# A changed opening: norms from token-major rows, modulation weights through GpSimd's queue, chains kept together, memory ahead of the context

## The chip, the core and the metric

The kernel runs on one core of a Trainium2 chip. A core has five engines that each work through their own list of instructions in order: TensorE (PE, matrix products), VectorE (DVE), ScalarE (ACT), GpSimd (POOL) and SyncE (SP, which here only issues DMAs). They wait for one another by semaphores. The metric is the device time of one execution in microseconds; lower is better. TensorE's clock as granted stands in the profile as a share of its full 2.4 GHz.

## The reference, cut to what matters

Two transformer-like blocks follow each other on 512 latent tokens of 1024 features, with 256 context tokens and 256 memory tokens:

```python
def first_block(x, c, ctx, c_ctx, ...):
    m_l = split(silu(c) @ ada_w + ada_b, 9)        # modulation of the latents
    m_c = split(silu(c_ctx) @ ada_w + ada_b, 9)    # modulation of the context
    x   = x   + 0.5 * m_l[2] * swiglu(modulate(rms_norm(x, norm1_w), m_l[0], m_l[1]), ffn1...)
    ctx = ctx + 0.5 * m_c[2] * swiglu(modulate(rms_norm(ctx, norm1_w), m_c[0], m_c[1]), ffn1...)
    y_l, y_c = token_mixing(...)                   # retention and gated linear attention
    x = x + m_l[5] * y_l
    x = x + 0.5 * m_l[8] * swiglu(modulate(rms_norm(x, norm3_w), m_l[6], m_l[7]), ffn2...)
    return rms_norm(x, final_norm_w)

def second_block(x, mem, ...):
    # dilated attention and a gated recurrence, then attention over the memory, then an MLP
    ... memory_cross_attention(rmsnorm(h, g), rmsnorm(mem, norm_mem_g), w_cq, w_ck, w_cv, w_co) ...

rms_norm(x, w) = x * rsqrt(mean(x * x over the features) + 1e-6) * w
```

The change concerns how the first block begins: the root-mean-square factors of x, ctx and mem, the modulation vectors (columns of `ada_w` times the activated condition), and the projections of the memory onto `w_ck` and `w_cv`, which the second block needs much later but which are made in the opening.

## The kernel before

All activations lie feature-major: eight tiles of 128 features by 512 (or 256) tokens. Every matrix product runs in three passes with operands split into a high and a low half (`wh`, `wl` of a weight; `hh`, `hl` of the latents, `h2` of the context and memory): high x high, high x low, low x high. ScalarE makes the high half by a copy, VectorE the low half by a subtraction (`split`, L446). A weight tile of 128x1024 is loaded by `wraw` (L434) on SyncE's queue into one of six places named `wr`, which all weights share; the modulation weights `ada_w` go there too.

The modulation: each 128 values of a modulation vector are one VectorE instruction (`tensor_tensor_reduce`, in the profile the custom instruction that writes `junk` and `mod`) over a 128x1024 tile of `ada_w` and the condition, which is replicated over partitions. `ada_first` (L655) does it for the first two vectors (shift and scale), 128 features at a time, and `ada` (L645) for the others.

The opening (L736 to L764) runs as follows. The condition, x and the memory are loaded. `rstd` (L526) finds the factors of a norm from the feature-major tiles: ScalarE squares them, VectorE adds the squares (`ss`), TensorE sums over the partitions by products with ones (`colsum`, into `st`), and VectorE computes the inverse root (`mean_eps` L516 and `rsqrt` L505: twelve small instructions one behind the other, `rsm`, `rsy`, `rst`). `spread` (L521) replicates the factors over partitions by TensorE (`rb`), and ScalarE copies them (`rbs`). `first_norm` (L708) takes eight steps, one per 128 features: two modulation products, the gain, `xn` = x times factor, the modulated halves `hh` and `hl`. After each step the up weights of FFN1 that have been loaded take the new features: seven units are begun in this loop (FIRST, L38). Two steps of the memory (`memory`, L679: four units of `w_ck`, two of `w_cv`) stand ahead of the loop and the rest behind it. Then FFN1 (`swiglu`, L810) goes on: for each up unit the latents' product, and from the seventh (ALONE, L37) also the context's; `ffn1_side` (L868) puts steps of other work beside each unit: `first_norm` of the context first, then the remaining modulation.

The order on each engine is not the order of the code. A planner (`Plan`, L143) records every operation with a cost and its dependences, and `issue` (L232) lists them: it takes the operation that can start first by its cost model, older ones first among equals, and keeps track of the places of each tile (`allowed`, L266; `pick`, L283). Every operation is put out by one line, so that nearly all of the profile's rows name L363.

Of the kernel before, what the change touches and what calls it, by code (L numbers as in the profile page):

```python
# [11 lines left out]
F32 = mybir.dt.float32  # L12
F32R = mybir.dt.float32r
I32 = mybir.dt.int32
# [4 lines left out]
P = 128  # L19
# [13 lines left out]
WBUFS = 5  # L33
TAIL = 3
# [108 lines left out]
class Plan:  # L143
# [9 lines left out]
    YIELD = 0.3  # L153

    def __init__(self, tc):
        self.tc, self.ops, self.caps, self.warm = tc, [], {}, False
# [13 lines left out]
    def add(self, name, engine, method, args, kwargs):  # L170
# [29 lines left out]
        self.ops.append((name, engine, method, args, kwargs, deps, tiles, cost, func))  # L200

    def cost(self, name, method, args, kwargs, outs, ins):
# [13 lines left out]
        if name == "SP":  # L216
            x = outs[0] if outs else ins[0]
            return int(np.prod(x.shape)) * 4 / 360.0 + 50
# [13 lines left out]
    def issue(self):  # L232
# [50 lines left out]
        def pick(e):  # L283
# [26 lines left out]
        while oldest < n:  # L310
# [5 lines left out]
            name, engine, method, args, kwargs, deps, tiles, cost, func = ops[i]  # L316
# [5 lines left out]
            landed = end + (2000 if e == "SP" else 0)  # L322
# [53 lines left out]
def tile_two_blocks(ctx: ExitStack, tc: tile.TileContext, a: dict, out: bass.AP, dbg=None):  # L376
# [128 lines left out]
    def rsqrt(m, cols):  # L505
        y = plan.tile(tp, [P, 32], F32, "rs_y", fresh("rsy"), 2)[:, :cols]
        t = plan.tile(tp, [P, 32], F32, "rs_t", fresh("rst"), 2)[:, :cols]
        V.tensor_scalar(y.bitcast(I32), m.bitcast(I32), 1, None, op0=ALU.logical_shift_right)
        V.tensor_scalar(y.bitcast(I32), y.bitcast(I32), -1, 0x5F3759DF, op0=ALU.mult, op1=ALU.add)
        for _ in range(3):  # L510
            V.tensor_mul(t, y, y)
            V.scalar_tensor_tensor(t, t, -0.5, m, op0=ALU.mult, op1=ALU.mult)
            V.scalar_tensor_tensor(y, t, 1.5, y, op0=ALU.add, op1=ALU.mult)
        return y

    def mean_eps(src, cols, scale):  # L516
        m = plan.tile(tp, [P, 32], F32, "rs_m", fresh("rsm"), 2)[:, :cols]
        V.tensor_scalar(m, src, scale, EPS, op0=ALU.mult, op1=ALU.add)
        return m
# [135 lines left out]
    def ada_first(c, s, k, junk):  # L655

        w = wraw(a["ada_w"][c, k], 1024)
# [21 lines left out]
    def memory():  # L679
# [81 lines left out]
    for _ in early:  # L761
        pass
    ctx_ = load(NC, "ctx", a["ctxT"])
    cond[1] = conditions(1)  # L764
# [901 lines left out]
def _arrange(inputs):  # L1666
# [3 lines left out]
    r["xT"], r["ctxT"], r["memT"] = _fm(g["x"][0]), _fm(g["ctx"][0]), _fm(g["mem_2"][0])  # L1670
# [81 lines left out]
```

## Time and profile before

| | |
|---|---|
| median of 3 runs | 2075.18 us (2071.36 to 2081.82) |
| the profiled execution | 2077.35 us |
| its span | 2075.5 us |
| TensorE busy | 2009.8 us, 97% |
| VectorE busy | 1190.4 us, 57% |
| ScalarE busy | 794.5 us, 38% |
| mean granted clock of TensorE | 0.981 |

The times are device times of whole executions; the profile is one more execution, and the span is the part of it between the first and last instruction. A row of the timeline gives the start, the length, the engine, the line, the operation, the tile written and the tiles read, and in brackets how long the engine had been idle ahead of it and what ended that.

### The profile page before, as it was taken

What the parts mean: (1) busy time and instruction counts of PE and PEld (TensorE: products, weight loads), DVE (VectorE), ACT (ScalarE), POOL (GpSimd) and SP (SyncE); (2) the same over time, 40 slices, a digit from 0 to 9 for tenths busy, and PEclk for the clock granted to TensorE, in tenths of its full rate; (3) what the DMA queues carried; (4) which work ended last, traced back from release to release, by engine and by line L of the source; (5) the groups of instructions that cost most, each with busy time, mean ns of one, the idle gap of its engine ahead of it and who ended that gap; (6) DMA issues with size and microseconds to landing.
All of it is one profiled execution on the core that took longest, in us unless ns stands there. A gap on an engine that the chain in (4) does not pass through costs nothing.

```text
span 2075.5 us, 27876 instructions
## 1 busy us (share of the span) xinstructions
PE 2009.8 (97%) x11033; PEld 1688.6 (81%) x11033; DVE 1190.4 (57%) x2157; ACT 794.5 (38%) x1238; POOL 121.1 (6%) x126
## 2 busy tenths in 40 slices
PE   5889999999999998999999999999998999999998
PEld 4779888888888876978988888888765888888887
DVE  7887844426247788589633333374866655343344
ACT  5452121221225654374432222343676363233231
POOL 0000000000000023110000000001243010000000
PEclk9989999999999999999999999999997999999999
DMA  8866624417132112232233323234321214333321
GB/s 312 270 236 199 196 77 140 145 60 224 51 107 94 45 52 72 67 91 83 71 117 101 97 92 104 86 94 124 85 74 27 64 59 132 101 92 102 93 70 41
DMA packets 73538, 225.57 MB, mean 109 GB/s; under 512 B 9360, under 2 KB 12096, under 8 KB 73408
## 3 DMA queue, kind: packets, MB, share of 16 engines
q1 hardware_dynamic: 73408, 223.80, 34.7%
q8 instruction: 86, 1.41, 0.3%
q14 instruction: 44, 0.36, 0.1%
HBM read 210.00 MB, written 5.24 MB: 104 GB/s over the span
## 4 chain that ended last, share of the span: by engine, by line
PE 87%; issue 5%; DVE 3%; DMA 2%; ACT 2%; POOL 1%; SPq 0%; DVEq 0%; ACTq 0%; POOLq 0%
PE p L363 77%; PE as L363 1%; PE gs L363 1%; PE ro L363 1%; PE rs L363 1%; PE at L363 1%; PE ao L363 1%; PE st L363 1%; PE go L363 1%; DVE junk L363 1%; DMA wr<-in_ffn_up_dram 1%; PE gl L363 1%; DVE rg_r L363 0%; PE rb L363 0%; POOL pg L363 0%
## 5 line engine op out<-in xcount | busy, mean ns | idle before, releaser
L363 ACT ACTIVATE wh<-wr 128x1024 fp32r<-128x1024 f32 (+4 forms) x295 | 298.2, 1012 | 751.1 <-PE p L363 566.1
L363 PE MATMUL p<-hh,wh 128*128 128x512 f32 (+1 forms) x1320 | 505.2, 389 | 13.2 <-ACT hh L363 7.9
L363 PE MATMUL p<-hl,wh 128*128 128x512 f32 (+1 forms) x1320 | 507.2, 388 | 0.0
L363 DVE TENSOR_TENSOR wl<-wr,wh 128x1024 fp32r<-128x1024 f32 (+4 forms) x295 | 345.9, 1177 | 170.7 <-ACT wh L363 77.6
L363 PE MATMUL p<-hh,wl 128*128 128x512 f32 (+1 forms) x1320 | 363.4, 387 | 4.3 <-DVE wl L363 4.3
L363 PE MATMUL p<-lo,wh 128*128 128x512 f32 (+1 forms) x831 | 310.0, 381 | 2.5 <-DVE lo L363 2.5
L363 PE MATMUL p<-hi,wh 128*128 128x512 f32 (+1 forms) x831 | 308.7, 380 | 2.0 <-ACT hi L363 2.0
L363 PEld LDWEIGHTS p<-hh,wh 128*128 128x128 f32 x1320 | 248.9, 190 | 57.6 <-ACT hh L363 10.4
L363 PEld LDWEIGHTS p<-hh,wl 128*128 128x128 f32 x1320 | 243.9, 190 | 54.5 <-DVE wl L363 4.7
L363 PEld LDWEIGHTS p<-hl,wh 128*128 128x128 f32 x1320 | 250.9, 191 | 37.5 <-issue 1.3
L363 PE MATMUL p<-hi,wl 128*128 128x512 f32 (+1 forms) x831 | 211.6, 375 | 0.0
L363 PEld LDWEIGHTS p<-lo,wh 128*128 128x128 f32 x831 | 158.6, 191 | 27.4 <-DVE lo L363 3.2
L363 PEld LDWEIGHTS p<-hi,wh 128*128 128x128 f32 x831 | 158.3, 191 | 24.4 <-ACT hi L363 2.2
L363 PEld LDWEIGHTS p<-hi,wl 128*128 128x128 f32 x831 | 148.8, 188 | 27.2
L363 PEld LDWEIGHTS p<-h,wh 128*128 128x128 f32 x816 | 138.8, 189 | 26.1
L363 DVE CUSTOM_DVE_ANT_0 junk<-wr,cond,vec 128x1024 f32<-128x1024 f32 x112 | 143.3, 1281 | 21.0 <-DMA wr<-in_ada_w_dram 20.1
L363 PE MATMUL p<-h,wh 128*128 128x256 f32 x816 | 145.5, 280 | 0.0
L363 DVE TENSOR_TENSOR act<-act,p 128x512 f32<-128x512 f32 (+1 forms) x68 | 38.3, 583 | 176.9 <-PE p L363 175.5
L363 DVE SCALAR_TENSOR_TENSOR x<-p,gate,x 128x512 f32<-128x512 f32 (+1 forms) x59 | 42.6, 723 | 106.0 <-PE p L363 106.0
L363 DVE TENSOR_TENSOR x<-p,x 128x512 f32<-128x512 f32 (+1 forms) x51 | 33.6, 658 | 112.9 <-PE p L363 112.7
L363 PE MATMUL p<-h,wl 128*128 128x256 f32 x408 | 97.3, 279 | 0.0
L363 PEld LDWEIGHTS p<-hid,wh 128*128 128x128 f32 x352 | 64.3, 188 | 14.3
(344 smaller groups left out, 2434.6 us busy)
## 6 DMA issues: line engine op xcount, KB each, us to landing
wr<-in_ffn_up_dram SPq DMA_DIRECT2D x100, 512.0 KB, 3.7
wr<-in_ada_w_dram SPq DMA_DIRECT2D x88, 512.0 KB, 4.4
wr<-in_mlp_up_dram SPq DMA_DIRECT2D x32, 512.0 KB, 3.6
wr<-in_mlp_dn_dram SPq DMA_DIRECT2D x32, 512.0 KB, 3.6
wr<-in_w_out_dram SPq DMA_DIRECT2D x16, 512.0 KB, 4.2
wr<-in_ffn_dn_dram SPq DMA_DIRECT2D x16, 448.0 KB, 3.2
wr<-in_ffn_dn_dram SPq DMA_DIRECT2D x16, 384.0 KB, 3.2
wr<-in_ffn_dn_dram SPq DMA_DIRECT2D x16, 320.0 KB, 2.8
```

Of the source, the lines that this page charges most:

```text
L363: ins = getattr(engine, method)(*args, **kwargs).ins
```

## The change

Token-major copies of x, ctx and mem are passed in beside the feature-major ones. `rstd_rows` loads 128 tokens at a time, and one ScalarE instruction squares a row and sums it (`accum_out`); VectorE's adds and TensorE's sums over ones are no longer needed for these three norms. The factor of x is computed first of all. `ada_w` tiles go through GpSimd's DMA queue into two places of their own (`wa`), and the weights keep four places `wr`. The chains of `rsqrt` and `mean_eps` are marked urgent for the planner. The memory's work moves from around the latents' loop to the sides of the first two FFN1 units, the context's loads and norm to the sides of the next three, and the remaining modulation behind them.

```diff
+RAWS = 4
+ARAWS = 2
...
+    RUSH = 200
+    LANDING = 2000
...
-        if name == "SP":
+        if method == "dma_start":
             x = outs[0] if outs else ins[0]
             return int(np.prod(x.shape)) * 4 / 360.0 + 50
...
+                rush = [c for c in cand if ops[c[1]][9] and c[0] - first <= self.RUSH]
+                if rush:
+                    return min(rush)
...
-    def wraw(ap, cols):
-        raw = plan.tile(wp, [P, 1024], F32, "wr", fresh("wr"), 6)
-        sync.dma_start(raw[:, :cols], ap)
+    def wraw(ap, cols, queue=sync, tag="wr", n=RAWS):
+        raw = plan.tile(wp, [P, 1024], F32, tag, fresh(tag), n)
+        queue.dma_start(raw[:, :cols], ap)
         return raw
+
+    def araw(c, j):
+
+        return wraw(a["ada_w"][c, j], 1024, G, "wa", ARAWS)
...
     def rsqrt(m, cols):
...
+        with plan.hurry():
+            V.tensor_scalar(y.bitcast(I32), m.bitcast(I32), 1, None, op0=ALU.logical_shift_right)
...
+    def rstd_rows(ap, n):
+
+        ss, junk = small(n // P, "ss"), wide4("junk")
+        for t in range(n // P):
+            S_.activation(junk, wraw(ap[t], 1024), AF.Square, accum_out=ss[:, t : t + 1])
+        return rsqrt(mean_eps(ss, n // P, 1.0 / D), n // P)
...
-            w = wraw(a["ada_w"][c, j], 1024)
+            w = araw(c, j)
...
-                y = rstd(mem.x)
+                y = rstd_rows(a["mem"], NC)
...
-    def first_norm(st):
-
-        rb = slot("rbs")[:, : st.n]
-        S_.activation(rb, rms_rstd(st.x), AF.Copy)
+    def first_factor(n, rows):
+        rb, made = bank("rb"), slot("rbs")[:, :n]
+        spread(rstd_rows(rows, n), n // P, rb)
+        S_.activation(made, rb[:, :n], AF.Copy)
+        return made
...
-    cond = [conditions(0), None]
+    latf = first_factor(NL, a["x"])
     lat = load(NL, "x", a["xT"])
     xt = lat.x
-    mem = load(NC, "mem", a["memT"])
-    early = memory()
-    for _ in range(2):
-        next(early)
-    normal = first_norm(lat)
+    cond = [conditions(0), None]
+    normal = first_norm(lat, latf)
...
-    for _ in early:
-        pass
-    ctx_ = load(NC, "ctx", a["ctxT"])
-    cond[1] = conditions(1)
+    mem = load(NC, "mem", a["memT"])
+    early = memory()
+    ctx_ = Stream(NC, None)
...
-    normal = first_norm(ctx_)
+    def second_norm():
+        ctx_.x = load(NC, "ctx", a["ctxT"]).x
+        factor = first_factor(NC, a["ctx"])
+        cond[1] = conditions(1)
+        yield from first_norm(ctx_, factor)
+
+    normal = second_norm()
...
-        if f < 4:
-            for _ in range(2):
+        if f < 2:
+            for _ in range(3 + f):
+                next(early, None)
+        elif f < ALONE - 1:
+            for _ in range(3):
                 next(normal, None)
-        else:
-            for _ in range(4 if f < 6 else 3):
+        if f >= ALONE - 2:
+            for _ in range(4):
                 next(rest, None)
```

How the instructions stand after it, in three places. First SyncE's queue behind the loads of x, before (`in_ada_w` are the modulation weights, `in_w_ck` the memory's weights, `in_ffn_up` those of FFN1):

```order
L363 DMA wr_132<-in_w_ck_dram 128x1024
L363 DMA wr_150<-in_w_ck_dram 128x1024
L363 DMA wr_168<-in_ada_w_dram 128x1024
L363 DMA wr_188<-in_ada_w_dram 128x1024
L363 DMA wr_219<-in_ffn_up_dram 128x1024
L363 DMA wr_245<-in_ffn_up_dram 128x1024
L363 DMA wr_263<-in_ada_w_dram 128x1024
L363 DMA wr_296<-in_ada_w_dram 128x1024
L363 DMA ctx_316<-in_ctxT_dram 128x512
```

The same queue behind the loads of x, now:

```order
L384 DMA cond_132<-in_cond_dram 128x1024
L384 DMA wr_137<-in_ffn_up_dram 128x1024
L384 DMA wr_145<-in_ffn_up_dram 128x1024
L384 DMA wr_152<-in_ffn_up_dram 128x1024
L384 DMA wr_162<-in_ffn_up_dram 128x1024
L384 DMA mem_169<-in_memT_dram 128x512
L384 DMA mem_179<-in_memT_dram 128x512
L384 DMA mem_181<-in_memT_dram 128x512
L384 DMA mem_189<-in_memT_dram 128x512
```

The modulation weights have left SyncE's queue, and the memory stands behind the first up weights. They are on GpSimd's queue now, from its start (MEMSET, ISA and AFFINE_SELECT make the identity matrix):

```order
masks.py:197 MEMSET ident_70 128x128
L384 DMA wa_81<-in_ada_w_dram 128x1024
masks.py:199 ISA
masks.py:199 AFFINE_SELECT ident_70<-ident_70 128x128
L384 DMA wa_85<-in_ada_w_dram 128x1024
L384 DMA wa_173<-in_ada_w_dram 128x1024
L384 DMA wa_187<-in_ada_w_dram 128x1024
```

Each load from the third on follows the instruction that has read the tile two before it. On VectorE, the first modulation products before (ISA rows that write `junk` are the products; `rst`, `rsy` end an inverse root, `ck` is the memory's projection):

```order
L363 TENSOR_TENSOR rst_280<-rsy_270 128x2
L363 SCALAR_TENSOR_TENSOR rst_280<-rst_280,rsm_265 128x2
L363 SCALAR_TENSOR_TENSOR rsy_270<-rst_280,rsy_270 128x2
L363 ISA junk_309,mod_310<-wr_168,cond_81,vec_79 128x1024
L363 ISA mod_310 128x1
L363 TENSOR_TENSOR ck_323<-p_185,fac_319 128x256
L363 TENSOR_TENSOR ck_323<-p_240,fac_319 128x256
L363 SCALAR_TENSOR_TENSOR gain_328<-mod_310,vec_79 128x1
L363 ISA junk_309,mod_332<-wr_188,cond_81,vec_79 128x1024
L363 ISA mod_332 128x1
L363 TENSOR_TENSOR xn_336<-x_83,rbs_321 128x512
L363 TENSOR_TENSOR wl_342<-wr_219,wh_278 128x1024
```

The same place on VectorE now:

```order
L384 TENSOR_TENSOR xn_154<-x_107,rbs_139 128x512
L384 TENSOR_TENSOR xn_156<-x_114,rbs_139 128x512
L384 TENSOR_TENSOR xn_158<-x_121,rbs_139 128x512
L384 ISA junk_164,mod_165<-wa_81,cond_132,vec_79 128x1024
L384 ISA mod_165 128x1
L384 SCALAR_TENSOR_TENSOR gain_171<-mod_165,vec_79 128x1
L384 ISA junk_164,mod_175<-wa_85,cond_132,vec_79 128x1024
L384 ISA mod_175 128x1
L384 TENSOR_TENSOR wl_183<-wr_137,wh_160 128x1024
L384 TENSOR_TENSOR wl_194<-wr_145,wh_167 128x1024
L384 TENSOR_TENSOR hl_206<-xn_141,hh_185 128x512
L384 ISA junk_164,mod_210<-wa_173,cond_132,vec_79 128x1024
```

The products of x and its factor (`xn`) stand ahead of the first modulation product, no other chain stands there, and a step holds two products that read the two places `wa`, then two low halves of weights and one of the latents (`hl`). Last, VectorE ahead of the context's units, before (`cond_81` and `cond_484` are the conditions of latents and context; the `wl` rows are low halves of FFN1's up weights, `act` begins a unit's activation):

```order
L363 ISA junk_1199,mod_1200<-wr_1155,cond_81,vec_79 128x1024
L363 ISA mod_1200 128x1
L363 ISA junk_1199,mod_1213<-wr_1155,cond_484,vec_79 128x1024
L363 ISA mod_1213 128x1
L363 ISA junk_1199,mod_1200<-wr_1173,cond_81,vec_79 128x1024
L363 ISA mod_1200 128x1
L363 ISA junk_1199,mod_1213<-wr_1173,cond_484,vec_79 128x1024
L363 ISA mod_1213 128x1
L363 TENSOR_TENSOR wl_1305<-wr_1187,wh_1218 128x1024
L363 TENSOR_TENSOR wl_1317<-wr_1202,wh_1232 128x1024
L363 TENSOR_TENSOR wl_1326<-wr_1221,wh_1248 128x1024
```

There now:

```order
L384 ISA junk_1319,mod_1338<-wa_1290,cond_287,vec_79 128x1024
L384 ISA mod_1338 128x1
L384 ISA junk_1319,mod_1320<-wa_1355,cond_132,vec_79 128x1024
L384 ISA mod_1320 128x1
L384 ISA junk_1319,mod_1338<-wa_1355,cond_287,vec_79 128x1024
L384 ISA mod_1338 128x1
L384 TENSOR_TENSOR wl_1389<-wr_1154,wh_1190 128x1024
L384 ISA junk_1319,mod_1320<-wa_1384,cond_132,vec_79 128x1024
L384 ISA mod_1320 128x1
L384 ISA junk_1319,mod_1338<-wa_1384,cond_287,vec_79 128x1024
L384 ISA mod_1338 128x1
L384 TENSOR_TENSOR wl_1407<-wr_1202,wh_1243 128x1024
```

The products of the third modulation vector stood in a block ahead of five low halves; now the low halves stand between the pairs of products, so that a low half waits on VectorE for what a pair in front of it waits for.

## Rows read from the trace of the kernel before

**Rows 1.** The page's first part: busy us (share of span) xinstructions of each engine.

```profile
PE 2009.8 (97%) x11033; PEld 1688.6 (81%) x11033; DVE 1190.4 (57%) x2157; ACT 794.5 (38%) x1238; POOL 121.1 (6%) x126
```

**Rows 2.** Windows: us, busy (count) of PE, PEld, DVE, ACT, POOL, PEclk, DMA, GB/s.

```profile
0.00:20.00 20.00, 6.44 (x29) 6.36 (x30) 10.44 (x26) 14.73 (x30) 0.70 (x6) 1.00 0.91 324
20.00:40.00 20.00, 13.82 (x71) 11.27 (x70) 17.90 (x47) 9.79 (x15) 0.00 (x0) 0.81 0.81 271
40.00:60.00 20.00, 18.20 (x72) 13.74 (x71) 17.17 (x30) 11.00 (x18) 0.00 (x0) 0.93 0.97 347
...
80.00:100.00 20.00, 17.41 (x147) 17.32 (x145) 16.51 (x41) 5.96 (x11) 0.00 (x0) 1.00 0.87 265
100.00:120.00 20.00, 11.38 (x32) 8.18 (x33) 16.44 (x35) 11.48 (x19) 0.00 (x0) 0.69 0.66 222
```

**Rows 3.** The chain of waits, pieces in order of time: start us, us, what.

```profile
118.33 500.83 PE p L363 x2942
```

**Rows 4.** Timeline of PE: start, us, engine, line, op, out<-in [idle before <-releaser].

```profile
69.90 0.39 PE L363 MATMUL p<-hl,wh 128*128 128x512 f32 x1
70.13 0.39 PE L363 MATMUL p<-hh,wl 128*128 128x512 f32 x1
...
79.19 2.08 PE L363 MATMUL p<-h,sh 128*128 128x256 f32 x16
81.11 1.12 PE L363 MATMUL p<-h,sl 128*128 128x256 f32 x8
...
113.48 3.06 PE L363 MATMUL p<-hh,wl 128*128 128x512 f32 x8 [4.26 <-DVE wl L363]
```

**Rows 5.** Windows over VectorE's stretch up to the context's fourth weight.

```profile
118.30:147.70 29.40, 29.37 (x146) 24.93 (x147) 25.70 (x38) 13.44 (x18) 0.00 (x0) 0.95 0.67 213
sum 121.30, PE 102.12 PEld 84.39 DVE 104.68 ACT 57.59 POOL 0.00; mean PE 34.04 PEld 28.13 DVE 34.89 ACT 19.20 POOL 0.00
```

**Rows 6.** Timeline of DVE, three stretches of the opening.

```profile
26.40 1.28 DVE L363 CUSTOM_DVE_ANT_0 junk<-wr,cond,vec 128x1024 f32<-128x1024 f32 x1
...
46.14 0.69 DVE L363 TENSOR_TENSOR xn<-x,rbs 128x512 f32<-128x512 f32 x1
46.74 1.22 DVE L363 TENSOR_TENSOR wl<-wr,wh 128x1024 fp32r<-128x1024 f32 x1
47.88 1.28 DVE L363 CUSTOM_DVE_ANT_0 junk<-wr,cond,vec 128x1024 f32<-128x1024 f32 x1
...
97.81 0.15 DVE L363 TENSOR_SCALAR rsm<-st 128x2 f32<-128x2 f32 x1
...
99.97 0.16 DVE L363 SCALAR_TENSOR_TENSOR rsy<-rst,rsy 128x2 f32<-128x2 f32 x1
...
139.88 5.76 DVE L363 TENSOR_TENSOR wl<-wr,wh 128x1024 fp32r<-128x1024 f32 x5
...
146.52 1.22 DVE L363 TENSOR_TENSOR wl<-wr,wh 128x1024 fp32r<-128x1024 f32 x1
```

**Rows 7.** Waits of SyncE's DMA queue, 0 to 150: waited for: us, times, longest.

```profile
SPq L363 <- DVE mod L363: 60.1, 28, 5.9
```

**Rows 8.** Timeline of ACT, first 32 us.

```profile
5.94 1.06 ACT L363 ACTIVATE cond<-cond 128x1024 f32<-128x1024 f32 x1 [3.92 <-DMA cond<-in_cond_dram]
...
27.79 0.59 ACT L363 ACTIVATE rbs<-rb 128x512 f32<-128x512 f32 x1
```

**Rows 9.** Groups by form, 0 to 200, DVE: busy us, mean ns | idle before.

```profile
L363 DVE CUSTOM_DVE_ANT_0 junk<-wr,cond,vec 128x1024 f32<-128x1024 f32 x54 | 69.1, 1279 | 3.7 <-DMA wr<-in_ada_w_dram 3.3
...
L363 DVE TENSOR_TENSOR ss<-ss,ss 128x256 f32<-128x256 f32 x12 | 5.0, 421 | 0.2
```

**Rows 10.** The page's sixth part: DMA issues, count, KB, median us to landing.

```profile
wr<-in_mlp_up_dram SPq DMA_DIRECT2D x32, 512.0 KB, 3.6
```

**Rows 11.** DMA issues from 0 to 150, same columns.

```profile
wr<-in_ada_w_dram SPq DMA_DIRECT2D x36, 512.0 KB, 5.2
...
x<-in_xT_dram SPq DMA_DIRECT2D x8, 256.0 KB, 6.1
```

More of the change, by code (lines that the diff above doesn't have):

```diff
@@ L153, with hurry, __enter__, __exit__ @@
     YIELD = 0.3
+    RUSH = 200
+    LANDING = 2000
     def __init__(self, tc):
-        self.tc, self.ops, self.caps, self.warm = tc, [], {}, False
+        self.tc, self.ops, self.caps, self.warm, self.urgent = tc, [], {}, False, False
+    def hurry(self):
+        plan = self
+        class Hurry:
+            def __enter__(self):
+                plan.urgent = True
+            def __exit__(self, *_):
+                plan.urgent = False
+        return Hurry()
     def engine(self, name, engine):
@@ L199, in add @@
         cost = self.cost(name, method, args, kwargs, outs, ins)
-        self.ops.append((name, engine, method, args, kwargs, deps, tiles, cost, func))
+        self.ops.append((name, engine, method, args, kwargs, deps, tiles, cost, func, self.urgent))
     def cost(self, name, method, args, kwargs, outs, ins):
@@ L315, in issue @@
             t0, i = c
-            name, engine, method, args, kwargs, deps, tiles, cost, func = ops[i]
+            name, engine, method, args, kwargs, deps, tiles, cost, func, _ = ops[i]
             if func is not None and table not in func:
@@ L321, in issue @@
             clock[e] = end
-            landed = end + (2000 if e == "SP" else 0)
+            landed = end + (self.LANDING if method == "dma_start" else 0)
             avail[e].remove(i)
@@ L507, in rsqrt @@
         t = plan.tile(tp, [P, 32], F32, "rs_t", fresh("rst"), 2)[:, :cols]
[L508 to L513, printed above, removed]
+        with plan.hurry():
+            V.tensor_scalar(y.bitcast(I32), m.bitcast(I32), 1, None, op0=ALU.logical_shift_right)
+            V.tensor_scalar(y.bitcast(I32), y.bitcast(I32), -1, 0x5F3759DF, op0=ALU.mult, op1=ALU.add)
+            for _ in range(3):
+                V.tensor_mul(t, y, y)
+                V.scalar_tensor_tensor(t, t, -0.5, m, op0=ALU.mult, op1=ALU.mult)
+                V.scalar_tensor_tensor(y, t, 1.5, y, op0=ALU.add, op1=ALU.mult)
         return y
@@ L517, in mean_eps @@
         m = plan.tile(tp, [P, 32], F32, "rs_m", fresh("rsm"), 2)[:, :cols]
-        V.tensor_scalar(m, src, scale, EPS, op0=ALU.mult, op1=ALU.add)
+        with plan.hurry():
+            V.tensor_scalar(m, src, scale, EPS, op0=ALU.mult, op1=ALU.add)
         return m
@@ L655, in ada_first @@
     def ada_first(c, s, k, junk):
-        w = wraw(a["ada_w"][c, k], 1024)
+        w = araw(c, k)
         V.tensor_tensor_reduce(junk, w, cond[s], 1.0, col("ada_b", NK * c + k), ALU.mult, ALU.add,
@@ L706, in memory, with first_norm @@
             sync.dma_start(md[:, i], t)
-    def first_norm(st):
-        rb = slot("rbs")[:, : st.n]
-        S_.activation(rb, rms_rstd(st.x), AF.Copy)
+    def first_factor(n, rows):
[3 more added lines that the diff above has]
+        return made
+    def first_norm(st, rb):
         s = 0 if st is lat else 1
@@ L863, in swiglu @@
             f0 += F
-    normal = first_norm(ctx_)
+    def second_norm():
[4 more added lines that the diff above has]
+    normal = second_norm()
     rest = (step for c in range(2, 9) for step in ada(c, (0, 1) if c < 5 else (0,)))
     def ffn1_side(f):
-        if f < 4:
-            for _ in range(2):
+        if f < 2:
+            for _ in range(3 + f):
+                next(early, None)
+        elif f < ALONE - 1:
+            for _ in range(3):
                 next(normal, None)
-        else:
-            for _ in range(4 if f < 6 else 3):
+        if f >= ALONE - 2:
+            for _ in range(4):
                 next(rest, None)
@@ L1669, in _arrange @@
     r = _constants()
-    r["xT"], r["ctxT"], r["memT"] = _fm(g["x"][0]), _fm(g["ctx"][0]), _fm(g["mem_2"][0])
+    for name, key in (("x", "x"), ("ctx", "ctx"), ("mem", "mem_2")):
+        r[name], r[name + "T"] = g[key][0].reshape(-1, P, D), _fm(g[key][0])
     vecs = np.zeros((P, NVEC), f32)
```

## The prediction

> **What bounds the kernel now.** The page's first part comes first: TensorE is busy for 97% of the span [rows 1], so a change to the opening can pay only where TensorE still waits. The windows say where: it lost 13.6 us of the first 20, 6.2, 1.8, 2.6 and 8.6 in the next stretches that have a row [rows 2], and the chain of waits has one piece without a gap from 118.33 on, 500 us long [rows 3]. I therefore measure everything in one number, the *lag*: the time at a point, less the TensorE work done by then. Work goes by the spacing of matmuls: 0.2265 us for 512 columns (one starts each 0.39 us bar, overlapped; 24 of them from the code make a unit of an up weight) and 0.120 us for 256 (sixteen from 79.19 to 81.11) [rows 4]. By 118.33 eight up units (8 x 24 x 0.2265 = 43.5) and the memory projections (192 x 0.120 = 23.0) are done: lag 118.33 - 66.5 = 51.8 us. The next 29.4 us run at a granted clock of 0.95 [rows 5], between the levels of 1.2 and 2.4 GHz, and cost 0.05 x 29.4 = 1.5 more: 53.3.
>
> Why so much? VectorE is the partner: from its first modulation product at 26.40 to the low half of the fourth context unit's weight, which ends at 147.7 [rows 6], it is busy 104.7 of 121.3 us [rows 5]. It is nearly gapless, and TensorE's last waits are for what comes out of that row, or for weights whose loads stood in SyncE's in-order queue behind a modulation load that waited for its place: 60.1 us of that queue's waiting is for the modulation products, and TensorE waited 4.26 us for a low half at 113.48 [rows 4, 7]. So the new time is the larger of two lags: VectorE's sum to the context units, and the latent loop's.
>
> **The start.** The factor of x now comes from token-major rows. Loads came as 0.63 MB landed by 5.94, when the condition's activation starts [rows 8], and at 324 GB/s in the first 20 us [rows 2]: an offset of 4.0. Ahead of the last row stand vectors 0.106, rows 2.10 and two modulation weights 1.05 MB: 4.0 + 3.26/0.324 = 14.1. Then a square of 1024 columns (1.06, as the condition's activation), the chain of twelve small operations, undisturbed (97.81 to 99.97 and 0.16: 2.3 [rows 6]), its spread by four small matmuls taken as 1.0, and the copy 0.59 [rows 8]: 19.1. Seven products x times factor, 0.60 each (46.14 to 46.74) [rows 6], now stand ahead: 23.3. The condition itself lands behind xT at 4.0 + 5.88/0.324 = 22.1, 23.2 after its activation. First modulation product at 23.4, 3.0 earlier than 26.40. In the kernel before, the chain was pulled apart by other work; it is now kept together, and that is inside this 3.0. The three smaller gains of the start (no adds of squares, no column sums on TensorE, four squares for eight) are inside it too: nothing else waits for them.
>
> **VectorE's sum to the same fourth context weight.** In the new order the memory's eight low halves (256 columns, 0.42 less 0.08 of overlap [rows 9], 2.8), its factor chain (2.3) and four low halves of 512 columns (0.60, 2.4) fall inside the stretch; seven xn products (4.2) and six adds of squares (2.1) leave it. 104.7 + 1.2 = 105.9, so it ends at 23.4 + 105.9 = 129.3 plus idle. TensorE has then, ahead of that weight's first use, twelve units of 512 columns (65.2), the memory (23.0) and 123 matmuls of 256 (14.8): 103.0. The lag is 26.3 + idle. It beats 53.3 while idle is under 27.0 us. Before, idle was 16.6 in this stretch.
>
> **The idle is the question: two places.** Modulation weights now have two places of their own and GpSimd's queue. A load can start only when the product of two before it has read the place. With L the time from issue to landing, one step (two products, one of each place) takes at least 1.20 (the product, 1.28 less 0.08 [rows 6]) + L + 0.1 for the semaphore. VectorE's own work in a latent step is 2 x 1.20, gain 0.06, two low halves at 1.14 [rows 6], and one of 512 columns at 0.60: 5.3; in a context step 5.6 on average over the new order. So idle begins at L = 4.0 and 4.3, and rises by 16 us for each us of L over the 16 steps, by about 18 with the eight products of the third modulation behind them. In the old order the same loads were mixed with others through six shared places, and VectorE waited 3.3 us for them in the first 200 [rows 9].
>
> L on this queue isn't in the trace. From below: the quietest loads of this size on SyncE's queue took 3.6 [rows 10]; from above, x's loads in the opening took 6.1; the modulation loads of the first 150 us took 5.2 [rows 11], in a ring shared with all else. I take 5.0, close to that nearest row: the ring now holds only these loads, but the 16 engines move 4 MB more rows in the opening (x 2.1, context 1.05, memory 1.05; 4.2/0.324 = 13 us of their time). Idle is then 8 x 1.0 + 8 x 0.7 = 13.6, 3 at the third modulation, and 6 of other waits (a third of the 16.6): 22.6. End 151.9, lag 48.9, gain 4.4 us. The profiled execution took 2077.35; 2072.9, and as that execution lies 2.2 over the median of 2075.18, about **2071**.
>
> The Trainium skill, DMA: Bandwidth & Descriptors (section Anatomy of one DMA — SWDGE (gpsimd) path), gives a load issued from GpSimd about 2.0 us plus its bytes over 436 GB/s; an estimate from it for 512 KB is 3.2 us, under every row here of that size. By it the steps never wait, and the time is the first rival's. The same page (section Latency and other measured facts) puts the first byte of such a load at about 1 us, against 0.6 for SyncE's, since software writes its descriptors: that speaks against this change. By it L would be 5.4, the idle 7 us more, and the time about 2078; no row before shows a load from GpSimd, so neither is borne out yet.
>
> **What else is moved.** SyncE's queue loses all modulation loads, so that up weights come when their places (four for six) are free: the 4.26 us wait [rows 4] should go; next late is VectorE's low half itself, already in the sum. The memory's 23.0 us of products move from beside the latent loop, where some filled TensorE's waits, behind it; that is in the lag, since the latent loop now counts without them. GpSimd's issuing of the loads lies beside nothing else of its own. ScalarE's squares (1.06 each, eight in all) lie in its idle time; if that cover were gone, 8.5 us. In later stages the shorter chains (rush rule) reshuffle mask and norm work: nothing, within 3 us either way, since a chain placed 200 ns earlier delays another operation as much.
>
> **Rivals.** *Full gain.* If L is at or under 4.4, VectorE is no longer last, and the latent loop decides. Before, its seven units were over at 79.19, where the memory's matmuls start [rows 4]; 3.0 earlier is 76.2, less 7 x 24 x 0.2265 = 38.1 of work: lag 38.1, gain 15.2, about **2060**. For it: 3.6 in the quiet loads. Against it: the DMA share of 0.66 to 0.97 in these windows [rows 2]. *Slower.* If L is 6.1, all sixteen steps wait for loads: 8 x 2.1 + 8 x 1.8 + 4 + 6 = 41 idle, end 170.5, lag 67.5, 14.2 worse: about **2089**. It decides from an idle of 27.0, L = 5.25 on. For it: loads at 6.1 and the extra rows; against it, that a ring of its own need not queue behind weights. *No effect of rows.* If the rows come late, because xT and the rows share the engines, the start is 26.4 again: 3 us of the gain go, about 2074; this lies inside the forecast's width.
>
> **How the numbers follow.** Forecast (L 4.6 to 5.5) 0.42, with 2063 to 2078 its own range; full gain 0.29; slower 0.24; something else, the later stages above all, 0.05. 0.5%, about what a measurement here can tell from no change, is 10 us: 2064.8 to 2085.6. Faster takes most of the full gain and a quarter of the forecast: 0.38. Slower takes most of its rival and a little of the forecast: 0.24. The same: 0.38. The range leaves a tenth out at each end: 2055 to 2092, past both rivals' prices by 3 to 5 us for the later stages.
>
> **What would show it.** Right: first modulation product near 23.4; loads from GpSimd landing in about 5 us; waits of VectorE for these loads of 1 us in each step, and TensorE gapless from about 120. Full gain: no such waits. Wrong: loads over 5.3 us, products spaced by L + 1.3 in pairs, TensorE waiting for low halves beyond 150 us; or a first product later than 26. A difference that arises after 200 us would break the whole argument.

## The result and the profile after

The changed kernel took 2090.91 us (median of 12 executions, 2083.42 to 2098.14), the kernel before 2078.3 beside it: ratio 1.0063, interval 1.0042 to 1.0083. It is slower, by 13 us; 2071 was forecast, a gain of 4.4 reckoned from 2075.18, the median of the three executions known then. Run again the ratio was 1.0048 (1.0028 to 1.0067).

The profiled execution took 2089.13 us, its span 2087.4. In the page's first part TensorE is busy as long as before [rows 1], so the time went into waits; a second queue has appeared in the third part:

```profile
PE 2009.3 (96%) x11001; PEld 1687.3 (81%) x11001; DVE 1182.9 (57%) x2139; ACT 796.6 (38%) x1231; POOL 169.6 (8%) x214
...
q1 hardware_dynamic: 61888, 181.85, 28.1%
q0 software_dynamic: 12672, 46.14, 6.9%
```

The windows answer to [rows 2]: the first 40 us hold 11.3 us of TensorE work (20.3 before), 80 to 120 are better than before, and 120 to 160, which were full before, lose 9.8 us at a granted clock of 0.91.

```profile
0.00:20.00 20.00, 2.04 (x8) 1.78 (x8) 3.84 (x16) 8.19 (x12) 1.92 (x8) 1.00 0.91 341
20.00:40.00 20.00, 9.22 (x28) 6.03 (x28) 15.20 (x24) 13.17 (x21) 2.64 (x5) 1.00 1.02 377
40.00:60.00 20.00, 19.02 (x70) 14.85 (x71) 15.01 (x34) 12.00 (x19) 2.64 (x5) 0.83 0.84 297
...
80.00:100.00 20.00, 20.00 (x162) 19.65 (x161) 15.19 (x36) 11.75 (x20) 1.58 (x3) 1.00 0.87 291
100.00:120.00 20.00, 17.64 (x91) 14.77 (x89) 13.89 (x28) 11.21 (x19) 2.64 (x5) 1.00 0.72 222
120.00:140.00 20.00, 17.31 (x82) 14.74 (x83) 17.02 (x31) 7.91 (x11) 3.28 (x7) 0.91 0.74 255
140.00:160.00 20.00, 12.85 (x97) 11.94 (x95) 16.97 (x27) 5.00 (x8) 3.06 (x6) 0.91 0.64 216
```

To compare openings whose work is ordered differently I use one marker: the first product of x with gain and factor for the second norm, which stands behind all of FFN1 and 400 us of gapless TensorE work. In the row of a tile, the last two numbers ahead of the forms are the starts of the first and last instruction. Before, and after:

```profile
L363 DVE SCALAR_TENSOR_TENSOR h<-x,gain,rb x32: 471/475/481, 623.5 to 1033.1; 128x256 f32<-128x256 f32 x32
```

```profile
L384 DVE SCALAR_TENSOR_TENSOR h<-x,gain,rb x32: 473/476/481, 628.9 to 1047.9; 128x256 f32<-128x256 f32 x32
```

The opening is 5.4 us longer by the marker. From the marker to the end of the span it is 1458.5 against 1452.0. So two losses are to be explained, and the second was not forecast at all.

TensorE's timeline after: the factor's spread starts at 15.58, the first main matmul at 26.10 (31.45 before); then come the waits for low halves up to 160, in place of the one at 113.48 in [rows 4].

```profile
15.58 2.04 PE L384 MATMUL rb<-ident,rsy 128*128 128x128 f32 x8 [15.58 <-DVE rsy L384]
26.10 2.59 PE L384 MATMUL p<-hh,wh 128*128 128x512 f32 x4 [8.47 <-ACT hh L384]
...
122.69 3.48 PE L384 MATMUL p<-hh,wl 128*128 128x512 f32 x8 [5.05 <-DVE wl L384]
...
156.02 1.76 PE L384 MATMUL p<-h,wl 128*128 128x256 f32 x8 [3.78 <-DVE wl L384]
160.04 2.07 PE L384 MATMUL p<-h,wl 128*128 128x256 f32 x8 [2.25 <-DVE wl L384]
```

VectorE's timeline, beside [rows 6], with the first product, two later ones that wait for their loads, and the low half of the fourth context unit's weight, the first of the pair at 158.76, which ends at 159.9:

```profile
22.51 1.28 DVE L384 CUSTOM_DVE_ANT_0 junk<-wa,cond,vec 128x1024 f32<-128x1024 f32 x1
23.72 0.08 DVE L384 DVE_READ_ACCUMULATOR2_ANT mod<- 128x1 f32 x1
23.83 0.16 DVE L384 SCALAR_TENSOR_TENSOR gain<-mod,vec 128x1 f32<-128x1 f32 x1
...
28.38 1.28 DVE L384 CUSTOM_DVE_ANT_0 junk<-wa,cond,vec 128x1024 f32<-128x1024 f32 x1 [0.32 <-DMA wa<-in_ada_w_dram]
...
37.56 1.28 DVE L384 CUSTOM_DVE_ANT_0 junk<-wa,cond,vec 128x1024 f32<-128x1024 f32 x1 [2.90 <-DMA wa<-in_ada_w_dram]
...
158.76 2.36 DVE L384 TENSOR_TENSOR wl<-wr,wh 128x1024 fp32r<-128x1024 f32 x2
```

GpSimd's timeline shows when the loads are issued. The first two start at 1.28 and 2.34; the third, into the place that the product of 22.51 read to 23.72, starts at 24.10, since its wait was for the gain behind that product:

```profile
1.28 0.72 POOL L384 DMA_DIRECT2D wa<-in_ada_w_dram  x1 [0.34 <-issue]
...
2.34 0.56 POOL L384 DMA_DIRECT2D wa<-in_ada_w_dram  x1
24.10 0.53 POOL L384 DMA_DIRECT2D wa<-in_ada_w_dram  x1 [21.21 <-DVE gain L384]
...
29.97 0.53 POOL L384 DMA_DIRECT2D wa<-in_ada_w_dram  x1 [3.96 <-DVE gain L384]
```

VectorE's waits from 22.5 to 160, the sum row of its windows, and two kinds of DMA issues up to 170:

```profile
DVE junk L384 <- DMA wa<-in_ada_w_dram: 21.0, 19, 4.4
```

```profile
sum 137.50, PE 114.28 PEld 96.85 DVE 108.47 ACT 66.24 POOL 19.00; mean PE 38.09 PEld 32.28 DVE 36.16 ACT 22.08 POOL 6.33
```

```profile
wa<-in_ada_w_dram POOLq DMA_DIRECT2D x38, 512.0 KB, 4.5
...
x<-in_xT_dram SPq DMA_DIRECT2D x8, 256.0 KB, 9.5
```

VectorE is busy 108.5 and idle 29.0 us in this stretch, 21.0 of it for modulation loads, in 19 waits. The loads landed in 4.5 us in the median, x's in 9.5 (6.1 before [rows 11]).

### The profile page after: what moved, and what is told of

Same layout as the page of the kernel before. It is cut to its first block, busy times and chain, and to the rows that moved or that the text cites. A ratio compares the mean times of both kernels' runs of the same rounds, so it can differ in the third digit from the quotient of the medians.

```text
span 2087.4 us, 27782 instructions
## 1 busy us (share of the span) xinstructions
PE 2009.3 (96%) x11001; PEld 1687.3 (81%) x11001; DVE 1182.9 (57%) x2139; ACT 796.6 (38%) x1231; POOL 169.6 (8%) x214
## 4 chain that ended last, share of the span: by engine, by line
PE 54%; issue 4%; DVE 2%; ACT 1%; POOL 1%; DMA 0%; SPq 0%; DVEq 0%; POOLq 0%; ACTq 0%
PE p L384 46%; PE as L384 1%; PE ro L384 1%; PE rs L384 1%; PE at L384 1%; PE ao L384 1%; PE go L384 1%; PE gs L384 0%; PE st L384 0%; DVE rg_r L384 0%; PE co L384 0%; PE orb L384 0%; PE ost L384 0%; ACT L384 0%; PE rb L384 0%
## 5 line engine op out<-in xcount | busy, mean ns | idle before, releaser
L384 PE MATMUL p<-hh,wh 128*128 128x512 f32 (+1 forms) x1320 | 503.0, 389 | 12.5 <-ACT hh L384 10.7
L384 DVE CUSTOM_DVE_ANT_0 junk<-wa,cond,vec 128x1024 f32<-128x1024 f32 x112 | 143.6, 1282 | 42.6 <-DMA wa<-in_ada_w_dram 41.8
L384 PEld LDWEIGHTS p<-h,wl 128*128 128x128 f32 x408 | 71.3, 195 | 6.6 <-DVE wl L384 6.5
```

Source lines behind the costliest of these rows:

```text
L384: ins = getattr(engine, method)(*args, **kwargs).ins
```

## The experiments

Each row gives the marker, the rest of the span behind it, and the ratio to the kernel before with its interval. "Places" are those of the modulation weights and of the others. "Spread" is the start of x's factor on TensorE. The marker and what lies behind it come from one profiled execution each, the ratio from the medians of all timed ones.

| kernel | issuer | places | spread | marker | behind it | ratio to before |
|---|---|---|---|---|---|---|
| before; again (e10) | SyncE | 6 shared | - | 623.5; 623.2 | 1452.0; 1454.4 | 1 |
| changed; again (e5) | GpSimd | 2 + 4 | 15.6; 15.2 | 628.9; 631.0 | 1458.5; 1462.6 | 1.0063; 1.0048 |
| e1; again (e11) | SyncE | 6 shared | 12.8; 12.5 | 619.5; 619.8 | 1453.4; 1453.0 | 0.9972 (0.9951 to 0.9993); 0.9968 (0.9954 to 0.9983) |
| e2; again (e12) | SyncE | 2 + 4 | 12.7; 12.6 | 617.9; 619.0 | 1464.5; 1456.4 | 0.9986 (0.9964 to 1.0008); 1.0001 (0.9986 to 1.0015) |
| e3 | GpSimd | 3 + 3 | 17.8 | 634.5 | 1454.6 | 1.0027 (1.0010 to 1.0045) |
| e4, not urgent | GpSimd | 2 + 4 | 15.9 | 630.0 | 1458.1 | 1.0013 (0.9991 to 1.0034) |
| e6 | GpSimd | 6 shared | 22.9 | 634.7 | 1446.0 | 1.0052 (1.0034 to 1.0071) |
| e7, one bus | GpSimd | 2 + 4 | 15.5 | 624.6 | 1455.9 | 1.0019 (1.0000 to 1.0038) |
| e8, rows alone | SyncE | 6 shared | 13.0 | 619.8 | 1450.1 | 0.9994 (0.9977 to 1.0011) |
| e9, one bus, held | GpSimd | 2 + 4 | 12.8 | 633.4 | 1463.5 | 1.0075 (1.0057 to 1.0094) |
| e13, SyncE's order | GpSimd | 2 + 4 | 15.2 | 628.1 | 1459.8 | 1.0056 (1.0038 to 1.0074) |
| e14, GpSimd's order | SyncE | 2 + 4 | 15.2 | 623.8 | 1460.3 | 1.0036 (1.0018 to 1.0054) |
| e15, SyncE's order | GpSimd | 6 shared | 15.0 | 623.1 | 1453.1 | 1.0010 (0.9992 to 1.0029) |
| e16 | SyncE | 4 shared | 12.9 | 632.5 | 1456.3 | 1.0053 (1.0033 to 1.0072) |
| e17, as e1, not urgent | SyncE | 6 shared | 12.8 | 619.5 | 1456.8 | 0.9974 (0.9955 to 0.9993) |

My first theory was the prediction's own mechanism, larger than I took it: two places hold the products back. The rivals were the queue itself, the later memory, and the urgent chains.

**e1, the modulation weights back on SyncE's queue in six shared places.**

```diff
-RAWS = 4
+RAWS = 6
-        return wraw(a["ada_w"][c, j], 1024, G, "wa", ARAWS)
+        return wraw(a["ada_w"][c, j], 1024)
```

> Only the modulation weights go back: SyncE's queue and six places shared with all weights; row norms, kept-together chains and the later memory stay. Marker for the opening: the first product of x with gain and factor for the second norm, 623.5 us before and 628.9 after the change. Theory (two places hold the products back): VectorE's 21 us of waits for these loads go down to under 6, and the marker comes at or ahead of 623. Rival (the memory's products no longer fill TensorE's waits in the latents' loop): the marker stays at 627 to 630. Rival (the later stages): whatever the marker does, the stretch behind it stays near 1458 us, as after the change, against 1452 before.

VectorE's wait fell to 3.7 us and the marker came 9.4 us earlier than after the change, 4.0 ahead of the kernel before. The later memory is cleared, and the stretch behind the marker was 1453.4, so that rival fell too. But queue and places changed together here. TensorE's last long wait of this opening is now for a high half, which ScalarE makes, and not for a low half of VectorE's, as after the change:

```profile
124.68 0.79 PE L384 MATMUL p<-hh,wh 128*128 128x512 f32 x1 [6.82 <-ACT wh L384]
```

**e2, own places, SyncE's queue.**

```diff
-        return wraw(a["ada_w"][c, j], 1024, G, "wa", ARAWS)
+        return wraw(a["ada_w"][c, j], 1024, sync, "wa", ARAWS)
```

> The two places of their own stay, but SyncE's queue issues the loads instead of GpSimd's. Theory (two places): the waits of VectorE for these loads stay at 15 to 30 us, since a place is free no earlier, and the marker stays at 627 to 635. Rival (the loads from GpSimd's queue are slow to start): the waits fall under 10 us and the marker comes ahead of 625.

The marker is 11 us ahead of the changed kernel's, as early as with six places, while VectorE still waited 12.6 us for these loads (0 to 200):

```profile
DVE junk L384 <- DMA wa<-in_ada_w_dram: 12.6, 17, 2.0
```

My theory fell in its plain form: with SyncE's queue two places cost nothing at the marker, and waits of VectorE for loads aren't by themselves lost time. By whole times e2 and e12 took 7.0 and 6.2 us longer than e1 and e11 timed beside them (medians 2082.20 and 2075.20, 2080.34 and 2074.16), so two own places, or the order that comes with them, did cost, but behind the marker.

**e3, three places each on GpSimd's queue.**

```diff
-RAWS = 4
-ARAWS = 2
+RAWS = 3
+ARAWS = 3
```

> GpSimd's queue stays, with three places for the modulation weights and three (for four) for the others, in the same memory. Theory (two places): the waits of VectorE for these loads fall from 21 to under 8 us and the marker comes 4 to 9 us ahead of 628.9, if three places are enough for the other weights; if these are short, SyncE's weights make TensorE or ScalarE wait instead, and the marker stays. Rival (the loads are slow or the DMA engines are full): the waits stay over 15 us.

The waits did fall, to 7.3 us, yet the marker came 5.6 later; three places for the up weights are too few to tell more. What it does show is the start: three loads go out on GpSimd at once, and TensorE's spread of the factor, in the same view as above, moves from 15.58 to 17.75.

```profile
DVE junk L384 <- DMA wa<-in_ada_w_dram: 7.3, 6, 2.3
```

```profile
17.75 2.05 PE L384 MATMUL rb<-ident,rsy 128*128 128x128 f32 x8 [17.75 <-DVE rsy L384]
```

**e4, no urgent chains.** The edit leaves `plan.urgent` at False.

> The chains are no longer marked urgent; all else as after the change. Theory (the opening is held up by the modulation loads alone): the marker stays within 3 us of 628.9. Rival for the later stages (the urgent chains reorder them): the stretch behind the marker falls from 1458.5 to about 1452, as before the change; if it stays at 1456 to 1460, the urgency isn't what costs there.

Marker 630.0: the urgency isn't what lengthens the opening. Behind the marker the profile has 1458.1, but this execution took 2089.89 us where the median of the twelve is 2083.31, and the ratio 1.0013 lies under the changed kernel's 1.0063 and 1.0048. So with two own places the urgency may cost something behind the marker. e17 does the same to e1:

> The first experiment without the urgent marking. Theory (the gain over the kernel before comes from the rows alone): 0.996 to 0.999 of before, marker at 618 to 621. Rival (the kept-together chains bring part of it): marker at 621 to 624, about 1.000.

The marker is e1's to the tenth, the ratio 0.9974: the gain over the kernel before isn't the chains'.

**e5, the changed kernel again, and e10, the kernel before again.**

> The changed kernel once more, with a profile of its own, beside the others of this set. Theory (the opening costs about 5 us by the marker, and what lies behind it differs from execution to execution by the granted clock): the marker within 3 us of 628.9, the stretch behind it anywhere from 1450 to 1462. Rival (the changed order of later work costs 6.5 us): the stretch behind it again 1458 to 1460.

> The kernel before the change once more, for a second profile. If the marker repeats within 2 us of 623.5 and the stretch behind it does not repeat within 2 us of 1452, the marker is the finer measure of the opening, and what differs behind it between single profiles is not an effect of a change.

The markers repeat within 2.1 and 0.3 us. Behind the marker the changed kernel was again longer: 1462.6, against 1454.4. But the same kernel differs there from profile to profile, by 2.4 and 4.1 us here and by 8.1 in e2 and e12, so these profiles alone don't show how much of the 4 to 11 us belongs to the change.

**e6, six shared places, GpSimd's queue.** The edit is e1's, with `G` as the queue.

> Six places shared with all weights, as before the change, but the modulation loads are issued by GpSimd; beside the first experiment only the queue differs. Theory (the second queue costs, not the two places): the marker at 626 to 634, as with two places, 7 to 14 us behind the first experiment's 619.5. Rival (the pair of two places and queue costs): the marker at 617 to 623.

With VectorE waiting only 3.5 us for these loads, this is the latest marker of all, 15 us behind e1. Five of GpSimd's loads now go out in the first 10 us, into places that x's rows need as well, and the spread starts at 22.91:

```profile
22.91 2.04 PE L384 MATMUL rb<-ident,rsy 128*128 128x128 f32 x8 [22.91 <-DVE rsy L384]
```

**e7, one bus in the plan.**

```diff
...
-                    cand.append((max(ready[i], w, clock[e]), i))
+                    bus = clock["bus"] if ops[i][2] == "dma_start" else 0.0
+                    cand.append((max(ready[i], w, clock[e], bus), i))
...
             clock[e] = end
+            if method == "dma_start":
+                clock["bus"] = end
...
```

> GpSimd's queue and two places stay; only the planner's model differs: the loads of both queues share one 360 GB/s instead of having that much each, so that it issues the memory's and the context's loads later. Theory (the plan counts the bandwidth twice, and loads that nobody needs yet take it from the modulation loads): the marker comes at 618 to 624, near the 617.9 of the SyncE queue with two places. Rival (the queue itself, by what GpSimd does before each load, holds the products back): the marker stays at 626 to 632.

624.6 lies between the two: 4.3 to 6.4 us ahead of the changed kernel, 6 behind the SyncE queue with two places. The planner's double bandwidth is a part, not all.

**e8, the rows alone.** To e1's edit is added: the memory's two calls go back around the latents' loop, the context's loads behind it.

> Of the change only the norms from rows (and the kept-together chains): SyncE's queue, six shared places, the memory around the latents' loop as before. Theory (the rows give an earlier start, about 5 us, that nothing takes back): the marker at 616 to 622, near the first experiment. Rival (the later memory is what the first experiment gained by): the marker at 622 to 626, as before the change.

619.8, e1's marker: of the change only the row norms gain, 3.6 us there, and the memory's later place neither gains nor costs at the marker. By whole times e8 can't be told from the kernel before.

**e9, the first two loads held.** To e7's edit is added:

```diff
...
+        if len(held) < 2:
+            held.append(G.tensor_copy(raw[:, :1], xt[7][:, :1]))
...
```

> As the experiment with one bus in the plan, and the first two loads of GpSimd's queue wait for x's last tile (a one-column copy from it into each place stands ahead of them), so that x's rows no longer share the engines with them. Theory (what the second queue costs is bandwidth taken at the wrong time): the factor's spread starts at 12.5 to 13.2 instead of 15.5, and the marker comes at 620 to 623, ahead of 624.6. Rival (the wait of each later load on GpSimd is what counts): the spread comes earlier, the marker stays at 624 to 627.

TensorE's spread is back at 12.81, yet the marker is 633.4. VectorE's timeline shows that the products gained nothing: the held loads landed only for 22.79, and the fourth product waited 3.31 us.

```profile
12.81 2.05 PE L388 MATMUL rb<-ident,rsy 128*128 128x128 f32 x8 [12.81 <-DVE rsy L388]
```

```profile
22.79 1.28 DVE L388 CUSTOM_DVE_ANT_0 junk<-wa,cond,vec 128x1024 f32<-128x1024 f32 x1 [2.36 <-DMA wa<-in_ada_w_dram]
...
33.23 1.28 DVE L388 CUSTOM_DVE_ANT_0 junk<-wa,cond,vec 128x1024 f32<-128x1024 f32 x1 [3.31 <-DMA wa<-in_ada_w_dram]
```

In the first 200 us VectorE waited 29.0 us for these loads, where e7 had 19.8 and the changed kernel 21.0; the order differs from e7's too. So this run refutes that an early factor suffices; it doesn't give a price.

**e13, e14 and e15: queue and order crossed.** The planner is told one engine and another issues the load, so that TensorE, VectorE and ScalarE keep an order word for word (e13; e14 has `"POOL", nc.sync`; e15 is e13's edit on e1):

```diff
+    mods = plan.engine("SP", nc.gpsimd)
...
-        return wraw(a["ada_w"][c, j], 1024, G, "wa", ARAWS)
+        return wraw(a["ada_w"][c, j], 1024, mods, "wa", ARAWS)
```

> Two own places; TensorE, VectorE and ScalarE have word for word the order of the kernel whose modulation loads SyncE issues (marker 617.9 and 619.0), but GpSimd issues these loads. Theory A (the second queue itself costs: its loads start ahead of x's rows and take a longer way round): marker at 626 to 632, spread of the factor at 15.5. Theory B (the planner, which gives each queue a bandwidth of its own, made the worse order): marker at 618 to 622.

> Two own places; TensorE, VectorE and ScalarE have word for word the changed kernel's order (marker 628.9 and 631.0), but SyncE issues the modulation loads, in the planned order between its other loads. Theory A (the queue): marker at 617 to 622. Theory B (the order): marker at 627 to 633, or later, as SyncE's loads now wait in line behind modulation loads whose places are taken.

> Six shared places; TensorE, VectorE and ScalarE have word for word the order of the first experiment (marker 619.5 and 619.8), but GpSimd issues the modulation loads. Theory A (the queue): marker at 625 or later. Theory B (the order): marker at 619 to 623, although the same queue with its own plan gave 634.7.

The markers, with the mean where there are two profiles:

| two own places | SyncE issues | GpSimd issues |
|---|---|---|
| SyncE's order | 618.5 | 628.1 |
| GpSimd's order | 623.8 | 630.0 |

Neither theory alone holds: the queue costs 9.6 or 6.2 us, the order 5.3 or 1.9, and the two overlap. Most of the overlap is the start: the spread comes at 12.7 and 12.6 only where SyncE issues in its own order, and at 15.2 to 15.6 in the other three. In e14 one queue does this alone, since its order puts two modulation loads among x's rows:

```profile
1.17 0.42 SPq L384 DMA_DIRECT2D wa<-in_ada_w_dram  x1
1.63 0.43 SPq L384 DMA_DIRECT2D wr<-in_x_dram  x1
2.10 0.43 SPq L384 DMA_DIRECT2D wa<-in_ada_w_dram  x1
2.58 1.48 SPq L384 DMA_DIRECT2D wr<-in_x_dram  x3
```

```profile
15.23 2.05 PE L384 MATMUL rb<-ident,rsy 128*128 128x128 f32 x8 [15.23 <-DVE rsy L384]
```

With six places and SyncE's order the queue costs only 3.4 (623.1 against 619.7), of which the start takes most, in TensorE's spread:

```profile
15.02 2.04 PE L384 MATMUL rb<-ident,rsy 128*128 128x128 f32 x8 [15.02 <-DVE rsy L384]
```

So at the marker it is the pair of queue and two places that costs: under GpSimd two places are 5.0 us worse than six (628.1 against 623.1), under SyncE 1.2 better. These are one or two profiles each, and repeats differ by up to 2.1.

**e16, four shared places on SyncE's queue.** e1 with `RAWS = 4`.

> As the first experiment (SyncE issues all loads), but four shared places instead of six. The part behind the marker is measured from the first to the last copy of the rotated queries in the mixing stage: 59.3 to 59.4 us in every profile of a kernel with six shared places, 60.3 or 63.2 in those with four places for the weights and two own. Theory (the four places left for the weights lengthen that stage): 60 to 63.5 there, and 1456 to 1464 from the marker to the end. Rival (the modulation loads' places don't reach that far; the clock alone differs): 59.4 there and 1450 to 1454. In the opening four places for everything should hold the up weights back: marker at 621 to 628.

The stage in question took 58.4 us, not over 60: four shared places don't lengthen it. The whole rest, 1456.3, lies at the lower edge of the theory's range, so the run is no clean answer. The opening is far worse than I expected, for another reason than before. The waits of 0 to 200 name it: TensorE for high halves, ScalarE for up weights (us, times, longest; e1 had 13.2 and 12.3 us).

```profile
PE p L384 <- ACT wh L384: 22.3, 5, 8.7
ACT wh L384 <- DMA wr<-in_ffn_up_dram: 19.0, 11, 5.7
```

## Why the prediction was wrong

**Start: right.** The first modulation product was forecast at 23.4 and came at 22.51; the last row came earlier than worked out (its square starts at 11.90, where 14.1 was reckoned for its landing), although the two loads of GpSimd stood ahead of it as reckoned. The spread, taken as 1.0 for four small matmuls, is eight and 2.04 us long; the two errors partly cancel, which is luck. What I didn't see is that this cost was part of the change: without them the spread comes at 12.7.

**VectorE's sum: nearly right.** 105.9 forecast, 108.5 measured, which is 2.6 of the 8.0 us by which its end came later than forecast; the place in the order, the low half of the fourth context weight, is where TensorE last waited, 2.25 us at 160.04.

**The step that failed** is "one step takes at least 1.20 + L + 0.1", with 5.0 for L. L itself was even shorter, 4.5 in the median. But what counts is the whole way from the end of the product that frees a place to the start of the product that waits for the next load in it: with the start of the product two before, plus 1.20, the ten waits before 104 us give 4.7 to 8.8, in the mean 6.1, where I had 5.1. GpSimd's load goes out 0.38 after the product's end, not 0.1, each issue takes GpSimd 0.53 us, and the loads that are waited for are the slow ones: the product at 37.56 waited for the one issued at 29.97, 7.6 earlier. No run splits the mean of 6.1 into these pieces. It is the 6.1 of the rival "Slower", as a way instead of a landing time. By this the idle was 29.0 where 22.6 was forecast (21.0 for 16.6 in the waits for modulation loads), the end 159.9 instead of 151.9, and with 103.0 of work the lag 56.9, 3.6 over 53.3; the marker says 5.4. The rival's idle of 41 and price of 14.2 were too high for the opening, and its total of 2089 is near the measured one only by luck, with what came behind.

A second step failed with it, "the new time is the larger of two lags: VectorE's sum to the context units, and the latent loop's". The full gain of 15.2 was to come once VectorE no longer waits and SyncE's queue is free of modulation loads. In e15, with six shared places, both nearly hold, with 4.7 us of such waits in 0 to 200, and yet its marker is that of the kernel before, with a start only 2.4 us later than e1's. What TensorE waited for last is a high half of an up weight, as in e1, a path that is neither of the two lags:

```profile
128.08 0.79 PE L384 MATMUL p<-hh,wh 128*128 128x512 f32 x1 [6.82 <-ACT wh L384]
```

No run here came to more than 6 us ahead of the kernel before at the marker.

**What the runs put in its place.** Added up at the marker, along one path: rows -3.6 (e8), later memory and urgent chains 0 (e1, e17), GpSimd as the issuer with the order kept +3.4 (e15), two own places under that queue +5.0 (e13; the order changes with them), GpSimd's own order +1.9 (the changed kernel): +6.7. Each step starts where the last one ends, so that this meets the +6.6 between the means of the two kernels' two profiles is no check; and with repeats up to 2.1 apart the last step isn't shown to differ from nothing. In the same order of work the way of a load, reckoned in the same manner, took 5.6 us under SyncE (e2, eight waits) and 6.7 under GpSimd (e13, nine). The landing itself was no slower: 4.9 and 4.8 in the median (0 to 170).

**"What else is moved."** For the opening the memory and the chains were rightly put at nothing. SyncE's queue lost its waits for modulation products, but not its long waits: it now waited for low halves that free its four places, fewer times than before [rows 7] and longer (0 to 150):

```profile
SPq L384 <- DVE wl L384: 64.7, 11, 15.7
```

The wait of 4.26 us that should go came back as 5.05 at 122.69. That low half starts at 121.42; ScalarE had made its last high half before it by 113.24. In VectorE's row it stood behind two products that had waited for their loads:

```profile
114.16 1.28 DVE L384 CUSTOM_DVE_ANT_0 junk<-wa,cond,vec 128x1024 f32<-128x1024 f32 x1 [4.44 <-DMA wa<-in_ada_w_dram]
...
119.80 1.28 DVE L384 CUSTOM_DVE_ANT_0 junk<-wa,cond,vec 128x1024 f32<-128x1024 f32 x1 [1.20 <-DMA wa<-in_ada_w_dram]
...
121.42 1.22 DVE L384 TENSOR_TENSOR wl<-wr,wh 128x1024 fp32r<-128x1024 f32 x1
```

So here the prediction's path, from a load through VectorE's row to TensorE, is seen as it was described. "Within 3 us either way" for the later stages failed: the two profiles of each kernel put 7 us there in the mean, about half of the whole loss, and a difference after 200 us was what the prediction said would break its argument. Between the first and the last of the marker's instructions lie 409.6 us before, 419.0 after and 426.6 in e5, and no more is lost behind them. In that stretch, in the mixing stage, the granted clock was lower after the change. The windows from 760 to 1000, before, after, the changed kernel again, and e1:

```profile
760.00:1000.00 240.00, 230.72 (x1413) 191.66 (x1412) 180.82 (x334) 118.53 (x185) 40.29 (x39) 1.00 0.26 77
```

```profile
760.00:1000.00 240.00, 230.06 (x1387) 188.94 (x1384) 174.46 (x320) 118.38 (x185) 48.26 (x52) 0.96 0.24 72
```

```profile
760.00:1000.00 240.00, 230.23 (x1373) 187.47 (x1373) 169.06 (x297) 114.87 (x180) 48.89 (x56) 0.92 0.24 69
```

```profile
760.00:1000.00 240.00, 232.20 (x1383) 191.59 (x1384) 176.32 (x327) 115.91 (x180) 39.61 (x38) 0.96 0.25 75
```

In the changed kernel TensorE's busy time is that of before, the clock 1.00, 0.96 and 0.92. But e1 has 0.96 as well, 417.2 us in that stretch, and still only 1453.4 from the marker to the end, so this window alone doesn't price the loss. Over the twelve timed executions of the changed kernel the clock went from 0.976 (2098.14 us) to 0.985 (2083.42). Which part of the order there lets the clock fall isn't settled: the window has 0.97 without the urgent marking (e4), 0.98 with four shared places (e16), and 0.94 in e2, the fastest at the marker. By whole times the loss behind the marker goes with the two own places and the order that they bring: beside the kernel with six shared ones theirs took 6.2 us longer under SyncE (e12, e11) and 11.4 under GpSimd (e13 2090.40, e15 2079.04), while the marker moved by -0.8 and 5.0. That leaves 6 to 7 us behind it in both pairs. How they do it isn't shown, and e4, with the same places and a ratio of 1.0013, says that they don't do it alone.

**The rule.** The Trainium skill, DMA: Bandwidth & Descriptors (section Anatomy of one DMA — SWDGE (gpsimd) path), gives such a load 2.0 us plus its bytes over 436 GB/s, an estimate of 3.2 for 512 KB, and with it a gain; the trace has 4.5, beside SyncE's loads on the same engines. In the same page of the Trainium skill (section Latency and other measured facts) the later first byte of GpSimd's loads pointed the right way, though its 0.4 us is not what the runs add up to, and no row here shows a first byte.

**The better version.** e1, the change without the move of the modulation weights, is faster than both kernels: 2074.16 us against 2078.46 for the one before in e11, ratio 0.9968 (0.9954 to 0.9983).

## What to carry to other kernels

Where few places hold a stream, count the whole way from the freeing instruction to the next use, and take the slow loads, not the median landing. A second DMA queue brought no bandwidth here (341 GB/s in the first 20 us, 342 with one queue in e2): what it could issue at the start went out at the start, needed or not, and delayed the first queue's loads. When a planner reorders everything, cross issuer and order before you blame either.

## What the runs showed of the hardware

Loads of 512 KB that GpSimd issued at the start delayed x's rows on SyncE's queue: with none, two and three of them (e2, the changed kernel, e3) the spread came at 12.7, 15.6 and 17.8, 1.4 to 1.7 us a load in the mean, and 0.524 MB at the 341 GB/s of the first 20 us is 1.54. It isn't the queue as such: with two such loads ahead on SyncE's own queue (e14) the spread came at 15.2. The Trainium skill, DMA: Bandwidth & Descriptors (section Issuing engines are not separate DMA queues), says that loads from all engines run on the same 16 DMA engines and interleave; the traces agree.
